# Hybrid decoder trunk: the first modulation's sums, their place before the first units, and the early constants

## The chip, the cores and the metric

The kernel runs on one core of a Trainium2 chip. Its time is the device time of one execution in microseconds (us); the number compared is the median of several executions. One core has five engines with queues of their own: TensorE (PE, with its weight loads shown apart as PEld), VectorE (DVE), ScalarE (ACT), GpSimd (POOL) and SyncE (SP), which here issues nearly all transfers. Each engine works through its queue in order and waits on semaphores of the others.

## The reference

One layer over 2048 positions of width 1024, then a final RMSNorm. Six modulation vectors come first, from the conditioning vector `c`:

```python
c_act = jax.nn.silu(c)
mod = c_act @ ada_w[l] + ada_b[l]                  # (1024) @ (1024, 6 * 1024)
sh1, sc1, g1, sh2, sc2, g2 = jnp.split(mod, N_MOD, axis=-1)
h = rmsnorm(x, norm_mix_w[l]) * (1.0 + sc1) + sh1
proj = h @ w_in[l]
...   # gated recurrence, top-k sparse attention, convolution; each on a slice of proj
x = x + g1 * (concat(o_a, o_b, o_c) @ w_out[l])
h = rmsnorm(x, norm_mlp_w[l]) * (1.0 + sc2) + sh2
x = x + g2 * (square(relu(h @ mlp_w1[l])) @ mlp_w2[l])
return rmsnorm(x, final_norm_w)
```

The change is about `sh1` and `sc1` (in the kernel `a1 = (1 + sc1) * norm_mix_w`), each a product of a vector of 1024 and a matrix of 1024 x 1024, without which no column of `h` can be made.

## The kernel before

The positions are worked in four blocks of 512. Per block, `in_block` makes the scaled and shifted activations transposed (eight tiles `k` of 128 x 512) and multiplies them with the columns of `w_in`, a unit of 128 or 256 columns at a time. Each float32 product is made from rounded parts: `whi`, `wlo` of the weights and `ah`, `al` of the activations, three matmuls for one. A unit of 128 columns is 24 matmuls of 128x512. What the units give feeds queues of background work (recurrence, convolution, indexer, top-k, attention), a bit of each after each unit. Later stages are the output product and the two MLP products.

The start. `in_norm(0)` loads four tiles `xt` and scales them. `ada_half(sec, c0, ...)` makes 512 columns of one modulation vector: it loads eight tiles `adw` (128 x 512, 256 KB each, one for each `k`), multiplies each by column `k` of `cact` and adds them up over `k`; then TensorE sums over the partitions, four matmuls with a moving vector of one column for each tile (`part_sum`). Of the eight tiles, before, DVE takes six (into `adacc`); for the two in `AK` ACT multiplies and POOL adds, and their sum goes through `part_sum` with `ones`. The halves `c0 = 0` for `a1` and `sh1` are needed for the tiles `k` = 0 to 3, the halves `c0 = TB` for `k` = 4 to 7.

`to_act_steps` makes one activation tile per step: four PE transposes into PSUM, `tf` on ACT (scale `a1`, shift `sh1`), `ah` on ACT, `al = tf - ah` on DVE or POOL. `tf` has two buffers, so the third `tf` waits until the first `al` is made. `first_units` begins two units (`KO = 2`, accumulators `at`) with `k` = 0 to 3 and ends them with `k` = 4 to 7. A third unit follows (accumulator `mm`, before `mm_661`), then a fourth (`mm_707`).

Weights come into two buffers `wraw`, are split by ACT (`whi`) and POOL (`wlo`), into four buffers each, and both parts are also written to DRAM (`wk_d`) for the later blocks.

The order in which each engine's queue stands is set by a scheduler when the program is built: it places the instructions by an estimated timeline of its own, with the order of the code as priority. So a change at the start can also move instructions much later.

`late_consts`, called after the second unit in block 0, makes the constants of the top-k search (`search_consts`: a few DVE operations on 14 columns, two powers on POOL) and five level masks (`lmask`: ten selections on POOL over 256 columns each, five copies on DVE).

Of the kernel before, what the change touches and what calls it, by code (L numbers as in the profile page):

```python
# [8 lines left out]
F32 = mybir.dt.float32  # L9
# [32 lines left out]
VB, GB, ZB = 3, 2, 3  # L42
HUB, FBB, HPM = 1, 2, 0
KO, NPF = 2, 2
AK = [1, 2]
PTB, PM, LB, LB2 = 1, 1, 4, 4
PREP = 14
R1 = [1126, 1216, 1594]
# [30 lines left out]
def trunk(ctx, tc, x, c, ada_w, ada_b, norm_mix_w, norm_mlp_w, w_in, hg_lb_logits,  # L79
# [136 lines left out]
    def ada_half(sec, c0, dst, key, slots):  # L216
        acc = hp.tile([P, TB], F32, tag="cu", bufs=2, name=nm("adacc"))
        pt = ps_ax()
        n = TB // P
        t0 = c0 // P  # L220

        side = []

        def part_sum(t, vec, first, last):
            for i in range(n):
                T.matmul(pt[:, i:i + 1], t[:, i * P:(i + 1) * P], vec, start=(first and i == 0),
                         stop=last, skip_group_check=True)

        for k in range(NK):
            t = slots[k]()  # L230
            dma(t, ada2[k * P:(k + 1) * P, sec * D + c0:sec * D + c0 + TB])
            if k in AK:
                A.mul(t, t, cact[:, k:k + 1])
                side.append(t)
                if len(side) > 1:
                    G.tensor_tensor(side[0], side[0], t, OP.add)
            elif k == 0:
                V.tensor_scalar(acc, t, cact[:, 0:1], None, op0=OP.mult)
            else:
                V.scalar_tensor_tensor(acc, t, cact[:, k:k + 1], acc, op0=OP.mult, op1=OP.add)  # L240
        if side:
            part_sum(side[0], ones[:, 0:1], True, False)
        part_sum(acc, ones[:, 0:1], not side, True)
        V.tensor_tensor(dst[:, t0:t0 + n], pt[:, :n], col("adab", sec * 8 + t0, n), OP.add)
        if key is not None:
            part = slice(c0 // P, (c0 + TB) // P)
            V.scalar_tensor_tensor(dst[:, part], dst[:, part], 1.0, cols[:, offs[key] + part.start:offs[key] + part.stop],
                                   op0=OP.add, op1=OP.mult)
# [23 lines left out]
        for i, j in zip(cuts, cuts[1:]):  # L272
            e.tensor_tensor(lo[:, i:j], src[:, i:j], hi[:, i:j].bitcast(F32), OP.subtract)  # L273

    def to_act_steps(xh, acol, bcol, ah, al, mid=None):
        for k in range(NK):
            guard = tc.high_priority(offset=HA)
            guard.__enter__()
            pt = {'0': ps_ax, '1': ps_mm, '2': ps_at, '3': ps_po}[(TA2 if px['ax'] < 3 else TA)[k]]()
            for t in range(4):  # L280
                T.transpose(pt[:, t * P:(t + 1) * P], xh[t][:, k * P:(k + 1) * P], ident)
            hi = ap.tile([P, TB], F32R, tag="ah", bufs=8, name=nm("ah"))
            lo = ap.tile([P, TB], F32R, tag="al", bufs=8, name=nm("al"))
            tf = xp.tile([P, TB], F32, tag="tf", bufs=2, name=nm("tf"))
            ac, bc = acol[:, k:k + 1], bcol[:, k:k + 1]
            A.activation(tf, pt, AF.Identity, scale=ac, bias=bc)  # L286
            A.copy(hi, tf)
            (V if k in (1, 4, 6) else G).tensor_tensor(lo, tf, hi.bitcast(F32), OP.subtract)
            guard.__exit__(None, None, None)
            ah.append(hi)  # L290
            al.append(lo)
            if mid is not None and k % 2:
                mid()
            yield
# [171 lines left out]
    def search_consts():  # L466
# [23 lines left out]
        G.iota(i8i, pattern=[[1, 8]], base=0, channel_multiplier=0)  # L490
        V.tensor_scalar(i8, i8i, 0.5, None, op0=OP.add)

    def late_consts():
        search_consts()
        cvrow = hp.tile([TAPS, 256], F32, tag="hc0", bufs=1, name="cvrow")
        nc.scalar.dma_start(cvrow, cv_w[0])
        pt = ps_ax()
# [7 lines left out]
        V.tensor_tensor(lbt, lbt, lbc, OP.mult)  # L505
        V.tensor_tensor(lbc, lbt, lbt, OP.subtract)
        V.tensor_scalar(oml, lbc, -1.0, 1.0, op0=OP.mult, op1=OP.add)

        mwork = hp.tile([P, 256], F32, tag="r", bufs=1, name="mwork")
        for l in range(5):  # L510
            h = 1 << l
            ng = 128 // (2 * h)
            V.memset(mwork, 1.0)
            G.affine_select(mwork, mwork, pattern=[[0, 4], [-2 * h, ng], [0, h]],
                            compare_op=OP.is_ge, fill=0.0, base=0, channel_multiplier=1)
            G.affine_select(mwork, mwork, pattern=[[0, 4], [2 * h, ng], [0, h]],
                            compare_op=OP.is_gt, fill=0.0, base=h, channel_multiplier=-1)
            V.tensor_copy(lmask[:, l, :], mwork)

    def ev_index_k(b, ps):  # L520
        full = st("stg", STG)
# [578 lines left out]

    def first_units(xts):
        act = [], []
        steps = to_act_steps(xts, a1, sh1, *act)
        ws = []
        for k in range(NK // 2):
            next(steps)
        for u in range(KO):
            ws.append(next_w())
            early.append(ps_at())
            mm_T(early[u], ws[u], act, True, None, 0, NK // 2)  # L1110
        ada_half(1, TB, a1, "nmix", far)
        ada_half(0, TB, sh1, None, far2)
        for _ in steps:
            pass
        for u in range(KO):
# [473 lines left out]
    far = [slot("f", ZB), slot("k", ZB), slot("q", ZB)] * 2 + [slot("v", VB), slot("gate", GB)]  # L1589
    far2 = [slot("f", ZB), slot("k", ZB), slot("q", ZB), slot("v", VB), slot("gate", GB)]  # L1590
    far2 += [slot("at", 2), slot("at", 2), slot("u", 2)]
    xq = [in_norm(0)]
    ada_half(1, 0, a1, "nmix", near)
    ada_half(0, 0, sh1, None, near)
# [74 lines left out]
```

## Time and profile before

| what | value |
|---|---|
| median of 3 runs (lowest to highest) | 2895.05 us (2892.56 to 2900.15) |
| the profiled execution | 2887.88 us, its span 2886.1 us |
| PE busy over the span | 2757.0 us, 96% |
| PE busy from 0 to 70 us | 40.40 us |
| PE busy from 70 to 200 us | 126.97 us |
| DVE, ACT, POOL busy over the span | 58%, 43%, 38% |
| mean granted TensorE clock | 0.987 |

Starts are counted in us from the first instruction. A row of the timeline reads: start, duration, engine, line, operation, output<-input, shapes, how many; in brackets the idle time ahead of it and what ended it. A float32 matmul of the kind of `part_sum` leaves two records, so four of them stand as x8.

### The profile page before, as it was taken

How to read it: one execution, taken by the hardware profiler on the slowest of the kernel's cores; microseconds unless marked ns; L12 is line 12 of the kernel's file. 1: busy time of each engine (PE TensorE's matmuls, PEld its weight loads, DVE VectorE, ACT ScalarE, POOL GpSimd, SP SyncE). 2: the span in 40 equal slices, each digit the busy share in tenths (PEclk: the TensorE clock that was granted, in tenths of full speed). 3: DMA queues.
4: the chain of work that ended last, by engine and by line, in shares of the span. 5: the costliest groups of instructions: out<-in, count | busy, mean ns of one | idle time of the engine just before them, and what ended most of it. 6: DMA issues, size and time to landing. Idle time of an engine off the chain costs nothing.

```text
span 2886.1 us, 42799 instructions
## 1 busy us (share of the span) xinstructions
PE 2757.0 (96%) x14116; PEld 2297.4 (80%) x14116; DVE 1671.6 (58%) x3514; ACT 1240.7 (43%) x2630; POOL 1086.6 (38%) x1051
## 2 busy tenths in 40 slices
PE   5999998999999989999999999999999999999997
PEld 4888887888788777888777888888788887777876
DVE  6695697777465437657757637477662221254455
ACT  4436444533311354555556444354643333343333
POOL 7434111212100445666665222234422223345444
PEclk9999999999999989999999999999999999999999
DMA  8987676777555667889888776677867666686676
GB/s 292 293 270 248 216 233 195 221 222 248 190 187 179 224 223 252 282 287 288 291 271 290 237 223 213 208 248 257 285 219 234 204 225 204 219 283 210 229 238 207
DMA packets 428075, 688.62 MB, mean 239 GB/s; under 512 B 43384, under 2 KB 171453, under 8 KB 427837
## 3 DMA queue, kind: packets, MB, share of 16 engines
q1 hardware_dynamic: 427680, 685.67, 73.0%
q8 instruction: 113, 1.85, 0.3%
q14 instruction: 126, 1.02, 0.1%
q10 hardware_dynamic: 156, 0.07, 0.0%
HBM read 532.74 MB, written 152.84 MB: 238 GB/s over the span
## 4 chain that ended last, share of the span: by engine, by line
PE 45%; DMA 4%; DVE 4%; POOL 2%; issue 1%; ACT 1%; SPq 0%; POOLq 0%; DVEq 0%; ACTq 0%
PE mm L1306 11%; PE mm L424 10%; PE ax L424 7%; PE ax L1306 6%; PE mm L1466 3%; PE at L967 2%; PE po L1001 2%; PE at L989 1%; PE ix L809 1%; DMA wk<-wk_d 1%; DMA tr<-in_mlp_w_dram 1%; PE at L1306 1%; DVE s L816 1%; POOL wk L376 1%; DVE cum L919 1%
## 5 line engine op out<-in xcount | busy, mean ns | idle before, releaser
L424 PE MATMUL mm<-ah,wk 128*128 128x512 f32 x1920 | 509.4, 396 | 4.9 <-ACT tf L286 1.9
L424 PEld LDWEIGHTS mm<-ah,wk 128*128 128x128 f32 x1920 | 353.6, 188 | 77.7 <-ACT tf L286 2.1
L318 POOL TENSOR_TENSOR wlo<-wraw,whi 128x512 fp32r<-128x512 f32 x210 | 286.7, 1385 | 243.4 <-ACT whi L317 99.7
L999 POOL TENSOR_TENSOR pT<-L,pT 128x512 fp32r<-128x512 f32 (+3 forms) x160 | 192.9, 1207 | 371.8 <-ACT pT L998 203.1
L816 DVE SCALAR_TENSOR_TENSOR s<-r,iw_s,s 128x512 f32<-128x512 f32 (+3 forms) x266 | 237.4, 892 | 100.9 <-ACT r L811 92.8
L424 PE MATMUL mm<-al,wk 128*128 128x512 f32 x960 | 262.3, 395 | 0.0
L969 DVE CUSTOM_DVE_ANT_0 L<-at,bias 128x512 f32<-128x512 f32 (+3 forms) x152 | 93.7, 620 | 202.5 <-PE at L967 159.3
L424 PEld LDWEIGHTS mm<-al,wk 128*128 128x128 f32 x960 | 177.9, 188 | 35.4
L1306 PE MATMUL mm<-wk,hh 128*128 128x512 f32 x640 | 196.0, 395 | 2.1 <-ACT tf L286 1.1
L811 ACT ACTIVATE r<-ix 128x512 f32<-128x512 f32 (+3 forms) x256 | 133.3, 555 | 148.8 <-PE ix L809 99.9
L317 ACT CAST whi<-wraw 128x512 fp32r<-128x512 f32 x210 | 121.8, 621 | 159.7 <-DMA wraw<-in_mlp_w_dram 40.1
L273 POOL TENSOR_TENSOR hl<-hr,hh 128x512 fp32r<-128x512 f32 x96 | 128.5, 1340 | 159.9 <-ACT hh L265 158.1
L424 PE MATMUL ax<-ah,wk 128*128 128x512 f32 x720 | 185.4, 391 | 1.8 <-ACT hc L1440 1.4
L589 DVE SCALAR_TENSOR_TENSOR cx<-hc,cvc,cx 128x512 f32<-128x512 f32 x232 | 174.2, 751 | 2.0
L919 DVE TENSOR_SCALAR_CACHE_REDUCE cum<-s,ssm 128x384 bf16<-128x384 f32 (+13 forms) x112 | 165.4, 1477 | 8.2 <-POOL s L820 6.1
L997 ACT COPY L<-at 128x512 f32<-128x512 f32 (+3 forms) x160 | 82.9, 522 | 175.6 <-PE at L989 174.2
L424 PEld LDWEIGHTS ax<-ah,wk 128*128 128x128 f32 x720 | 134.1, 188 | 30.2 <-ACT hc L1440 1.8
L1466 PE MATMUL mm<-wk,hc 128*128 128x512 f32 x588 | 145.0, 392 | 6.9 <-DVE acc L1474 6.1
L983 ACT ACTIVATE L<-L,nmx 128x512 f32<-128x512 f32 (+3 forms) x160 | 103.8, 650 | 98.7 <-DVE nmx L978 98.4
L1306 PEld LDWEIGHTS mm<-wk,hh 128*128 128x128 f32 x640 | 118.0, 188 | 26.8 <-ACT tf L286 1.7
L1466 PEld LDWEIGHTS mm<-wk,hc 128*128 128x128 f32 x588 | 109.4, 188 | 34.1 <-DVE acc L1474 10.0
L1306 PE MATMUL ax<-wk,hh 128*128 128x512 f32 x384 | 122.6, 397 | 1.5 <-DMA wk<-wk_d 1.1
(364 smaller groups left out, 6077.8 us busy)
## 6 DMA issues: line engine op xcount, KB each, us to landing
wk<-wk_d SPq DMA_DIRECT2D x776, 256.0 KB
wk<-wk_d SPq DMA_DIRECT2D x196, 512.0 KB
wk_d<-whi SPq DMA_DIRECT2D x210, 256.0 KB
wk_d<-wlo SPq DMA_DIRECT2D x210, 256.0 KB
wraw<-in_mlp_w_dram SPq DMA_DIRECT2D x68, 512.0 KB
kc<-sk_d SPq DMA_DIRECT2D x112, 256.0 KB
vc<-v_d SPq DMA_DIRECT2D x112, 256.0 KB
adw<-in_ada_w_dram SPq DMA_DIRECT2D x128, 128.0 KB
```

Source lines behind the costliest of these rows:

```text
L273: e.tensor_tensor(lo[:, i:j], src[:, i:j], hi[:, i:j].bitcast(F32), OP.subtract)
L317: A.copy(hi, src)
L318: G.tensor_tensor(lo, src, hi.bitcast(F32), OP.subtract)
L424: T.matmul(ps, ww[k], aa[k], start=(n == 0 and k0 == 0), stop=(n == len(order) - 1 and k1 == NK))
L589: V.scalar_tensor_tensor(acc if w < TAPS - 1 else total, hc[:, w:w + TB], cvc[:, m, w:w + 1], acc, op0=OP.mult, op1=OP.add)
L811: A.activation(r[:, :w], ps[:, :w], AF.Relu, scale=32.0 ** -0.5)
L816: V.scalar_tensor_tensor(s[:, c0:c0 + w], r[:, :w], iw, s[:, c0:c0 + w], op0=OP.mult, op1=OP.add)
L919: V.tensor_scalar(dump, s, t, -AIM - i * STEP, op0=OP.is_ge, op1=OP.add, accum_out=d)
L983: A.activation(lt[:, :w], lt[:, :w], AF.Exp, bias=nmx, accum_out=sm[:, cb:cb + 1])
L999: G.tensor_tensor(pT[:, :nt, 1], lv, pT[:, :nt, 0].bitcast(F32), OP.subtract)
L1306: T.matmul(ps, aa[f][:, tok * P:(tok + 1) * P], ww[i], start=(first and n == 0), stop=(last and n == 5))
L1466: T.matmul(bank[t], aa[:, k, t * P:(t + 1) * P], ww[k], start=(i in (0, 2, 4) and n == 0), stop=(n == 5), skip_group_check=True)
```

## The change

Four edits:

- `AK` is `[2, 5]` instead of `[1, 2]`, and for these two of the eight tiles TensorE multiplies by `cact` itself: `part_sum(t, cact[:, k])` accumulates into the same PSUM tile. ACT's eight multiplications and POOL's four additions go; each of the four halves has twelve `part_sum` matmuls instead of eight.
- The two `ada_half` calls for the second half stand ahead of the first two units in `first_units`, no longer behind their first half.
- In block 0, all eight `al` are made on DVE, before three of eight (the other blocks keep 1, 4, 6).
- `search_consts` and the level masks (now `level_masks`, 64 columns selected and copied four times) stand at the very start, ahead of the load of `x`, no longer in `late_consts`.

```diff
-AK = [1, 2]
+AK = [2, 5]
...
             if k in AK:
-                A.mul(t, t, cact[:, k:k + 1])
-                side.append(t)
-                if len(side) > 1:
-                    G.tensor_tensor(side[0], side[0], t, OP.add)
+                part_sum(t, cact[:, k:k + 1], k == AK[0], False)
...
-        if side:
-            part_sum(side[0], ones[:, 0:1], True, False)
-        part_sum(acc, ones[:, 0:1], not side, True)
+        part_sum(acc, ones[:, 0:1], False, True)
...
-            (V if k in (1, 4, 6) else G).tensor_tensor(lo, tf, hi.bitcast(F32), OP.subtract)
+            (V if k in on_v else G).tensor_tensor(lo, tf, hi.bitcast(F32), OP.subtract)
...
+    def level_masks():
+        mwork = hp.tile([P, 5, 64], F32, tag="r", bufs=1, name="mwork")
+        V.memset(mwork, 1.0)
+        for l in range(5):
...
+            G.affine_select(mwork[:, l], mwork[:, l], pattern=[[-2 * h, ng], [0, h]],
...
+        for c in range(4):
+            V.tensor_copy(lmask[:, :, c * 64:(c + 1) * 64], mwork)
...
     def late_consts():
-        search_consts()
...
     def first_units(xts):
         act = [], []
-        steps = to_act_steps(xts, a1, sh1, *act)
+        steps = to_act_steps(xts, a1, sh1, *act, None, range(NK))
         ws = []
         for k in range(NK // 2):
             next(steps)
+        ada_half(1, TB, a1, "nmix", far)
+        ada_half(0, TB, sh1, None, far2)
         for u in range(KO):
             ws.append(next_w())
             early.append(ps_at())
             mm_T(early[u], ws[u], act, True, None, 0, NK // 2)
-        ada_half(1, TB, a1, "nmix", far)
-        ada_half(0, TB, sh1, None, far2)
...
+    search_consts()
+    level_masks()
     xq = [in_norm(0)]
```

What the scheduler makes of it, at three places. First PE's queue at the second half's sums: `adacc_427`, `adw_469`, `adacc_464` are the second half before (`ax_428` for `a1`, `ax_465` for `sh1`), `adacc_413`, `adw_459`, `adw_471`, `adacc_451` the same now (`ax_414`, `ax_452`); `at_...` are the matmuls of the first two units, `mm_511` and `mm_542` transposes of the second half. Before:

```order
L226 MATMUL ax_428<-ones,adacc_427 128x1
L424 MATMUL at_391<-al_368,whi_375 128x512
L424 MATMUL at_391<-ah_367,wlo_376 128x512
L424 MATMUL at_414<-al_368,whi_383 128x512
L424 MATMUL at_414<-ah_367,wlo_384 128x512
L226 MATMUL ax_465<-ones,adw_469 128x1 x4
L226 MATMUL ax_465<-ones,adacc_464 128x1 x4
L281 MATMUL mm_511<-ident,xt_213 128x128
```

Now, on the same engine at the same work:

```order
L274 MATMUL mm_542<-ident,xt_251 128x128
L417 MATMUL at_506<-al_397,whi_490 128x512
L224 MATMUL ax_414<-ones,adacc_413 128x1 x4
L224 MATMUL ax_452<-cact,adw_459 128x1 x4
L224 MATMUL ax_452<-cact,adw_471 128x1 x4
L224 MATMUL ax_452<-ones,adacc_451 128x1 x4
L417 MATMUL at_506<-ah_396,wlo_491 128x512
L417 MATMUL at_506<-ah_407,whi_490 128x512
```

The last sum of the modulation has moved ahead of nine matmuls of the units' first half (`at_506`, `at_529`, with `k` = 2 and 3), which before stood ahead of it.

Second, DVE's queue in the second half of the modulation (`adacc_427` then `adacc_464` before, `adacc_413` then `adacc_451` now; `al_346` and `al_375` to `al_408` are the low parts of `k` = 0 to 3). Before:

```order
L518 CAST lmask<-mwork 128x256
L240 SCALAR_TENSOR_TENSOR adacc_427<-adw_439,cact,adacc_427 128x512
L240 SCALAR_TENSOR_TENSOR adacc_427<-adw_442,cact,adacc_427 128x512
L240 SCALAR_TENSOR_TENSOR adacc_427<-adw_445,cact,adacc_427 128x512
L288 TENSOR_TENSOR al_346<-tf_347,ah_345 128x512
L240 SCALAR_TENSOR_TENSOR adacc_427<-adw_448,cact,adacc_427 128x512
L238 TENSOR_SCALAR adacc_464<-adw_466,cact 128x512
L240 SCALAR_TENSOR_TENSOR adacc_427<-adw_451,cact,adacc_427 128x512
L240 SCALAR_TENSOR_TENSOR adacc_464<-adw_476,cact,adacc_464 128x512
```

Now:

```order
L235 SCALAR_TENSOR_TENSOR adacc_413<-adw_427,cact,adacc_413 128x512
L281 TENSOR_TENSOR al_375<-tf_376,ah_374 128x512
L281 TENSOR_TENSOR al_386<-tf_387,ah_385 128x512
L235 SCALAR_TENSOR_TENSOR adacc_413<-adw_430,cact,adacc_413 128x512
L235 SCALAR_TENSOR_TENSOR adacc_413<-adw_439,cact,adacc_413 128x512
L281 TENSOR_TENSOR al_397<-tf_398,ah_396 128x512
L235 SCALAR_TENSOR_TENSOR adacc_413<-adw_442,cact,adacc_413 128x512
L233 TENSOR_SCALAR adacc_451<-adw_453,cact 128x512
L281 TENSOR_TENSOR al_408<-tf_409,ah_407 128x512
L235 SCALAR_TENSOR_TENSOR adacc_451<-adw_456,cact,adacc_451 128x512
```

All four low parts now stand between the twelve modulation steps, before one did; the masks and search constants are gone from here.

Third, POOL's queue from the third of the four first weight splits (`wlo`) on. Before:

```order
L318 TENSOR_TENSOR wlo_384<-wraw_327,whi_383 128x512
L318 TENSOR_TENSOR wlo_388<-wraw_327,whi_387 128x512
L236 TENSOR_TENSOR adw_432<-adw_432,adw_435 128x512
L288 TENSOR_TENSOR al_335<-tf_336,ah_334 128x512
L288 TENSOR_TENSOR al_357<-tf_358,ah_356 128x512
L236 TENSOR_TENSOR adw_469<-adw_469,adw_472 128x512
L288 TENSOR_TENSOR al_368<-tf_369,ah_367 128x512
L479 TENSOR_TENSOR sconst<-sconst 128x14
```

Now:

```order
L311 TENSOR_TENSOR wlo_499<-wraw_367,whi_498 128x512
L311 TENSOR_TENSOR wlo_503<-wraw_367,whi_502 128x512
L311 TENSOR_TENSOR wlo_522<-wraw_488,whi_521 128x512
L311 TENSOR_TENSOR wlo_526<-wraw_488,whi_525 128x512
L247 TENSOR_SCALAR rs_2326<-ss_2324 128x1
```

Between the splits of the first two units and those of the third, POOL has nothing left to do.

More of the change, by code (lines that the diff above doesn't have):

```diff
@@ L220, in ada_half @@
         t0 = c0 // P
-        side = []
         def part_sum(t, vec, first, last):
@@ L273, in low_part, with to_act_steps @@
             e.tensor_tensor(lo[:, i:j], src[:, i:j], hi[:, i:j].bitcast(F32), OP.subtract)
-    def to_act_steps(xh, acol, bcol, ah, al, mid=None):
+    def to_act_steps(xh, acol, bcol, ah, al, mid=None, on_v=(1, 4, 6)):
         for k in range(NK):
@@ L491, in search_consts @@
         V.tensor_scalar(i8, i8i, 0.5, None, op0=OP.add)
+    def level_masks():
+        mwork = hp.tile([P, 5, 64], F32, tag="r", bufs=1, name="mwork")
+        V.memset(mwork, 1.0)
+        for l in range(5):
+            h = 1 << l
+            ng = 128 // (2 * h)
+            G.affine_select(mwork[:, l], mwork[:, l], pattern=[[-2 * h, ng], [0, h]],
+                            compare_op=OP.is_ge, fill=0.0, base=0, channel_multiplier=1)
+            G.affine_select(mwork[:, l], mwork[:, l], pattern=[[2 * h, ng], [0, h]],
+                            compare_op=OP.is_gt, fill=0.0, base=h, channel_multiplier=-1)
+        for c in range(4):
+            V.tensor_copy(lmask[:, :, c * 64:(c + 1) * 64], mwork)
     def late_consts():
-        search_consts()
         cvrow = hp.tile([TAPS, 256], F32, tag="hc0", bufs=1, name="cvrow")
@@ L507, in late_consts @@
         V.tensor_scalar(oml, lbc, -1.0, 1.0, op0=OP.mult, op1=OP.add)
[L509 to L518, printed above, removed]
     def ev_index_k(b, ps):
```

## The prediction, as it was put on record

> **What bounds the kernel now.** I read the page first, then the busy times by stage, then those of the first 120 us, and then each engine's timeline from 20 to 70 us. The columns behind the stretch are its length, busy time (records) of PE, PEld, DVE, ACT and POOL, granted clock, DMA share, GB/s.
>
> ```profile
> span 2886.1 us, 42799 instructions
> core 0: us, PE busy (x) PEld busy (x) DVE busy (x) ACT busy (x) POOL busy (x), PEclk, DMA share, GB/s
> 0.00:70.00 70.00, 40.40 (x173) 32.81 (x174) 47.65 (x92) 34.01 (x57) 51.47 (x54) 0.98 0.89 291
> 70.00:200.00 130.00, 126.97 (x706) 109.91 (x705) 99.39 (x242) 51.00 (x103) 59.02 (x52) 0.99 0.87 276
> 200.00:1000.00 800.00, 772.62 (x4683) 663.76 (x4683) 538.80 (x1317) 312.51 (x732) 168.61 (x204) 0.99 0.68 217
> 1000.00:2886.00 1886.00, 1816.98 (x8560) 1490.90 (x8558) 985.70 (x1864) 843.21 (x1739) 807.51 (x742) 0.99 0.74 243
> ```
>
> From 70 us on PE is idle only 3.0 + 27.4 + 69.0 us of 2816; before that it is idle 29.6 of 70. So what a change of the start is worth is how much earlier PE becomes busy for good; everything later hangs on PE and moves with it, but for what the DMA queue cannot bring earlier. When does that happen, and what is it waiting for?
>
> ```profile
> 30.52 0.16 DVE L244 TENSOR_TENSOR sh<-ax,cols 128x4 f32<-128x4 f32 x1 [1.40 <-PE ax L226]
> 50.19 0.16 DVE L244 TENSOR_TENSOR sh<-ax,cols 128x4 f32<-128x4 f32 x1 [0.91 <-PE ax L226]
> ...
> 27.94 1.14 ACT L317 CAST whi<-wraw 128x512 fp32r<-128x512 f32 x2 [1.15 <-DMA wraw<-in_w_in_dram]
> 30.78 1.45 ACT L286 ACTIVATE tf<-mm,sh,a 128x512 f32<-128x512 f32 x2 [1.70 <-DVE sh L244]
> 39.38 0.78 ACT L286 ACTIVATE tf<-mm,sh,a 128x512 f32<-128x512 f32 x1 [4.91 <-DVE al L288]
> 58.70 0.78 ACT L286 ACTIVATE tf<-mm,sh,a 128x512 f32<-128x512 f32 x1 [4.04 <-DVE gq__210 L488]
> 59.51 0.62 ACT L287 CAST ah<-tf 128x512 fp32r<-128x512 f32 x1
> ...
> 60.17 0.50 PE L424 MATMUL mm<-ah,whi 128*128 128x512 f32 x1 [3.75 <-ACT ah L287]
> 69.44 1.98 PE L424 MATMUL mm<-ah,whi 128*128 128x512 f32 x8
> ```
>
> The reader is to see a chain: first half of the modulation done at 30.7, second half at 50.35, last activation tile `ah` at 60.13, and from there PE never stops. Unit four (mm_707) begins at 69.44; that is my checkpoint. Two stalls stand on the chain besides the modulation: `tf` waits 4.91 us for a low part, and 4.04 us for DVE's search constants. Why the second half comes only at 50:
>
> ```profile
> 28.75 0.37 DVE L238 TENSOR_SCALAR adacc<-adw,cact 128x512 f32<-128x512 f32 x1
> 32.50 5.11 DVE L240 SCALAR_TENSOR_TENSOR adacc<-adw,cact,adacc 128x512 f32<-128x512 f32 x3
> 37.53 1.75 DVE L288 TENSOR_TENSOR al<-tf,ah 128x512 fp32r<-128x512 f32 x1
> 40.27 7.26 DVE L240 SCALAR_TENSOR_TENSOR adacc<-adw,cact,adacc 128x512 f32<-128x512 f32 x6
> ...
> 31.17 4.22 POOL L318 TENSOR_TENSOR wlo<-wraw,whi 128x512 fp32r<-128x512 f32 x3
> 35.35 1.71 POOL L236 TENSOR_TENSOR adw<-adw,adw 128x512 f32<-128x512 f32 x1
> 37.02 1.72 POOL L288 TENSOR_TENSOR al<-tf,ah 128x512 fp32r<-128x512 f32 x1
> 48.78 2.60 POOL L479 TENSOR_TENSOR sconst<-sconst 128x14 f32<-128x14 f32 x1 [2.59 <-DVE sconst L476]
> ...
> L240 DVE SCALAR_TENSOR_TENSOR adacc<-adw,cact,adacc x20: 716/750/1758, 12.8 to 46.8; 128x512 f32<-128x512 f32 x20
> L288 DVE TENSOR_TENSOR al<-tf,ah x3: 683/691/1754, 37.5 to 57.9; 128x512 fp32r<-128x512 f32 x3
> ```
>
> DVE works without a break from 28.75 to 47.5, and beside POOL's tensor_tensor its steps take 1.70 us (5.11 for three) where the median is 0.75.
>
> **The change part by part.**
>
> *First half, TensorE's quarter.* The eight ACT multiplications and four POOL additions go; DVE keeps its six tiles a half. `tf` at 30.78 waited 1.70 us for `sh`; ahead of it on ACT stand the weight casts, which end at 29.08 and wait for DMA, whose issue order is the same now. So the gain here is between 0 and 1.7 us. I take 1.7, since DVE no longer waits between its steps for POOL's masks.
>
> *The early constants.* POOL now does ten selections of 64 columns and two powers at the start, instead of ten selections of 256 spread over it:
>
> ```profile
> 2.17 2.12 POOL L514 TENSOR_SCALAR_AFFINE_SELECT mwork<-mwork 128x256 f32<-128x256 f32 x1
> ```
>
> At most ten of this row are 21 us, at a quarter each 5.3, beside 5.2 for the two powers at 2.60; POOL is then free for `rs` (the norm of `x`) between 12.7 and, at worst, 28. The transposes need the scaled `x` by 29: hidden, so I cost it at nothing; the worst end would cost about 2 us. What it takes away is the 4.04 us wait at 58.70.
>
> *Second half ahead of the units, all low parts on DVE.* DVE now owes from about 28.3: ten steps of 0.75, two of 0.4, four `al` of 0.69, that is 11.1 us; about two of them run beside POOL's remaining `wlo` and take 1.70 (2.0 more). The end is 41.4, against 47.5. It cannot be before the last tile lands. Landed by then must be 4 x 0.52 MB of x, 32 x 0.26 of ada_w and 1.05 of weights, 11.6 MB:
>
> ```profile
> 0.00:10.00 10.00, 0.24 (x1) 0.17 (x1) 1.97 (x15) 2.20 (x3) 6.86 (x13) 1.00 0.79 273
> 10.00:20.00 10.00, 3.15 (x13) 2.57 (x13) 7.35 (x15) 7.65 (x14) 9.04 (x11) 1.00 0.93 321
> 20.00:30.00 10.00, 6.08 (x28) 5.48 (x27) 8.54 (x17) 2.34 (x5) 6.03 (x7) 1.00 0.98 269
> 30.00:40.00 10.00, 5.53 (x21) 4.24 (x20) 8.87 (x8) 4.32 (x7) 8.73 (x7) 1.00 1.06 390
> ```
>
> 8.63 MB by 30 us and 0.39 MB per us after: 37.6. So the sums are DVE's, with 3.8 us to the floor. PE then does four matmuls:
>
> ```profile
> 31.61 1.97 PE L281 MATMUL mm<-ident,xt 128*128 128x128 f32 x8 [1.13 <-ACT tf L286]
> 28.62 1.86 PE L226 MATMUL ax<-ones,adacc 128*128 128x1 f32 x8 [2.89 <-DVE adacc L240]
> 49.12 1.03 PE L226 MATMUL ax<-ones,adacc 128*128 128x1 f32 x8
> 41.55 0.63 PE L424 MATMUL at<-ah,wlo 128*128 128x512 f32 x1
> 41.98 0.63 PE L424 MATMUL at<-ah,whi 128*128 128x512 f32 x1
> 44.17 0.39 PE L424 MATMUL at<-ah,whi 128*128 128x512 f32 x1
> 44.41 0.40 PE L424 MATMUL at<-al,whi 128*128 128x512 f32 x1
> 62.00:64.00 2.00, 2.00 (x6) 1.60 (x5) 0.75 (x1) 1.81 (x4) 0.45 (x2) 0.50 0.95 268
> ```
>
> PE's queue now holds the last sum ahead of nine unit matmuls, so it will have waited since about 38; after a wait of this kind the trace shows 0.43 us from matmul to matmul (41.55 to 41.98), later 0.24 (44.17 to 44.41), and 1.86 for the four small ones against 1.03. I take the slow ones: sums at 43.3, `sh` at 43.5, a gain of 6.8 (bounds: 10.5 at the DMA floor with quick sums; 5 if two more steps meet POOL). The sixteen more small matmuls lie in such waits but for the last eight, counted here.
>
> The granted clock behind the 3.75 us wait of before is 0.50 (62 to 64 us). The Trainium skill (TensorE: Matmul & The Clock Gate, Part 1) says that PE's clock halves after an idle window of about 3.4 us and is full again after as long of sustained work; that speaks against placing the last sum ahead of the nine matmuls. By it the next step costs what I take from the rows; without it the checkpoint would be 2.4 us earlier. The trace agrees at 62 us; at 41.98 its column says 1.00 where the matmuls are slow, so there the rows decide.
>
> *From `sh` to the checkpoint.* Ahead of the first `tf` of the second half now stand, on PE, the nine matmuls (0.43 each) and seven transposes (0.25, eight in 1.97): 43.3 + 3.9 + 1.7 = 48.9. Two `tf` (1.45 as at 30.78) and two `ah` (1.14 as the casts at 27.94) follow; the first `ah` is at 50.9, its `al` on DVE at 51.6, and as DVE has no constants in between, the last `ah` at 54.3 (60.13 before, with the 4.04 in it). PE is busy for good from 51.6: 46 matmuls at 0.227 (eight take 1.98 us, the last 0.39 of it: 1.59 in seven steps) bring unit four at 62.1. Against 69.44 that is 7.3 us.
>
> *The transfers.* They must do in 62 us what they did in 69.4.
>
> ```profile
> 104.24 1.14 ACT L317 CAST whi<-wraw 128x512 fp32r<-128x512 f32 x2 [3.05 <-DMA wraw<-in_w_in_dram]
> 100.00:110.00 10.00, 10.00 (x51) 8.57 (x50) 8.56 (x15) 4.16 (x9) 5.82 (x4) 1.00 0.99 299
> ```
>
> 20.2 MB (291 GB/s x 69.4) against 12.5 MB by 40 us and 22 us at 0.33 (between the rows' 0.30 and 0.39): about 0.4 MB short, 1.1 at 0.30, so 1 to 3.5 us of backlog, part of it x for the next block that nobody awaits. The split at 104.24 waits for DMA, just ahead of its use. I take 1 us off, with 0 and 3.5 as bounds. Sum: 7.3 - 1 = 6.3, say 6.5 us with the small relief of DVE behind it. On the profiled execution 2886.1 - 6.5 = 2879.6 us of span, 2881.4 with the 1.8 around it; the median of the runs is 7.2 above the profiled execution, so 2895.05 - 6.5 = 2888.5.
>
> **The rivals.**
>
> *Quick clock and no cover lost.* If PE stays at full clock there, unit four comes 2.4 us earlier, and if the DVE steps meet POOL less, up to 3 more. Against it: the slow rows at 41.55. Gain 9 to 13, 2882 to 2886.
>
> *DMA takes it back.* If each unit's weights come at the pace of the saturated queue (share 0.99 at 100 to 110), unit four begins when 20.2 MB have come, 12.5 by 40 us and the rest at 0.30 MB/us: 66 us, a gain of 3.5, or 1 to 4 with what waits behind it, 2891 to 2894. Against it: PE is 10.00 of 10 there and never waited.
>
> *Slower.* The scheduler writes the queues of blocks 0 to 3 in another order. PE is idle 27.4 us from 200 to 1000, in small waits, and DVE is 538.8 of 800 busy there. If the new order puts PE's matmuls ahead of the DVE results they need, these waits grow; they must reach 43 us (27.4 + 6.5 + 8.7) for a slower kernel: 2904 or more. For it: nothing binds this order to what DVE can do. Against it: the order of the work is the code's, only shifted.
>
> **How the numbers follow.** A difference under 0.3%, 8.7 us, cannot be told from none. Forecast (gain 4 to 9) 0.45, of which 0.05 is over 8.7; quick 0.32; DMA 0.12; slower 0.11, of which 0.02 is within 0.3%. That makes faster 0.37, same 0.54, slower 0.09. The range goes from a gain of 13 (2882) to a loss of 3 (2898): it leaves out the slower rival and a little of the quick one.
>
> **What would show it.** `sh` of the second half near 43.5, last `ah` near 54, unit four near 62, and PE idle from 70 to 1000 about 30 us as before: right. `sh` before 41 says the contention was over-counted; matmuls at 0.24 right after the last sum, that the clock was. If the checkpoint is early and the end is not, the waits between 200 and 1000 or casts waiting for `wraw` took it.

## The result, and the profile after

The changed kernel takes 2918.15 us (median of 6 runs, 2914.95 to 2920.16); the kernel before takes 2897.6 beside it on the same chip (6 runs, 2884.49 to 2903.12). The ratio is 1.0071, 95% interval 1.0055 to 1.0087: slower by 20.5 us, where the prediction was 6.5 us faster and its range ended at 2898.

The busy times by stage of the changed kernel (columns as in the prediction: PE, PEld, DVE, ACT, POOL, granted clock, DMA share, GB/s):

```profile
span 2918.5 us, 42856 instructions
0.00:70.00 70.00, 49.53 (x228) 42.55 (x229) 43.65 (x92) 28.76 (x49) 30.03 (x46) 0.95 0.91 302
70.00:200.00 130.00, 122.31 (x677) 105.18 (x676) 100.57 (x246) 51.07 (x102) 53.15 (x49) 0.97 0.85 264
200.00:1000.00 800.00, 766.92 (x4580) 659.17 (x4579) 533.10 (x1299) 311.70 (x727) 152.21 (x195) 0.97 0.66 211
```

The start is better: PE is busy 49.5 us of the first 70, before 40.4. From 70 to 200 us PE is idle 7.7 us instead of 3.0, from 200 to 1000 33.1 instead of 27.4, and the granted clock there is 0.97 instead of 0.99. Two things follow: PE waits 10.4 us more (40.8 against 30.4), and it is slower while it works.

To see where the time goes I matched every TensorE instruction of the two profiled executions (same line, same tiles, same count) and took the start after minus the start before, the median in each stretch of the kernel before:

| stretch of before, us | 75–150 | 200–450 | 500–550 | 600–675 | 800–1000 |
|---|---|---|---|---|---|
| lag of the changed kernel, us | -2.7 | +1.7 | +3.7 | +8.6 | +20.3 |

So the start's gain is 2.7 us at 75 us, and 23.0 us are lost between 150 and 760 us; from there to 1000 us the lag does not move. For the work between 150 and 760 us PE waits 25.1 us before and 33.8 now (there 147.3 to 780.4 us), so waits explain 8.7 of these 23.0; the other 1.7 of the 10.4 lie ahead of it, at 73 us. The remaining 14.3 is the same matmuls taking longer. The trace's clock records show half clock (granted clock 0.50) for 51.2 us between 70 and 1000 us (nine stretches), before for 17.1 (four), and all of these lie between 150 and 765 us. The split is that of two single executions, and that of before has little half clock: the two other kernels below with its queues have 27.3 and 34.1 us of it.

(The profiled executions differ by 32.3 us in all. That of before, 2887.88, stands 9.7 under the median beside it, that of the changed kernel 2.0 over its own; 9.7 + 2.0 + 20.5 is the 32.3. Behind 1000 us the lag grows by another 9 us; it also grows by 7 us or more in two of the kernels below that are not slower, the fill on the kernel before and TensorE's quarter alone.)

The waits of PE from 70 to 1000 us, summed by what PE waited for (total, times, longest), first the kernel before, then the changed one:

```profile
PE mm L281 <- ACT tf L286: 5.8, 7, 1.8
PE ax L671 <- DVE r L751: 4.6, 4, 3.0
...
PE ax L696 <- DVE k L662: 1.6, 2, 1.0
...
```

```profile
PE mm L274 <- ACT tf L279: 6.4, 7, 1.7
PE mm L417 <- DVE slo L535: 6.0, 1, 6.0
PE at L1007 <- POOL ot L1005: 3.4, 2, 3.1
PE ax L690 <- DVE k L656: 3.2, 2, 2.5
...
```

Three long waits are new: 6.0 us for `slo`, 3.1 for `ot`, 2.5 for `k`. All three come from the new order: something late stands ahead of what PE needs, or what PE needs hangs on a transfer that has moved back. The first, in the changed kernel on DVE and PE, and behind it a window of busy time:

```profile
164.29 0.14 DVE L927 CAST far<-at 1x1 uint32<-1x1 f32 x1
170.01 1.50 DVE L872 SCALAR_TENSOR_TENSOR s<-cum,s 128x384 f32<-128x384 bf16 x1 [4.84 <-DVEq L930]
175.81 0.68 DVE L535 SCALAR_TENSOR_TENSOR slo<-mm,shi 128x512 fp32r<-128x512 f32 x1
176.55 3.78 PE L417 MATMUL mm<-ah,whi 128*128 128x512 f32 x8 [5.98 <-DVE slo L535]
176.50:182.50 6.00, 5.95 (x14) 4.75 (x15) 6.00 (x18) 0.38 (x1) 0.00 (x0) 0.50 0.58 171
```

L930 is a branch on a value that the search computes (`far`); DVE stands 4.84 us there. `slo` frees the PSUM bank (a part of the memory into which PE writes its sums) that PE needs next, and in the new order it stands behind the branch and behind a piece of the search, so PE waits 5.98 us; then eight matmuls take 3.78 us instead of 1.98 at clock 0.50. In the kernel before, `slo` stands ahead of its branch and is done 9 us earlier:

```profile
166.96 0.68 DVE L541 SCALAR_TENSOR_TENSOR slo<-mm,shi 128x512 fp32r<-128x512 f32 x1
176.75 0.56 DVE L878 SCALAR_TENSOR_TENSOR s<-cum,s 128x384 f32<-128x384 bf16 x1 [5.80 <-DVEq L936]
```

The second, at 575 us: on ACT a load of its function table (1.28 us) and a `cu` of the convolution stand right ahead of the copy `ot`, which POOL and then PE need:

```profile
573.76 0.72 ACT L615 ACTIVATE cu<-cacc,cols 128x512 f32<-128x512 f32 x1
575.33 0.48 PE L1007 MATMUL at<-ident,ot 128*128 128x128 f32 x1 [3.06 <-POOL ot L1005]
```

In the kernel before, this `cu` stands ahead of the exponentials `L` and not between them and `ot`, and PE does not wait for `ot`:

```profile
562.88 0.74 ACT L621 ACTIVATE cu<-cacc,cols 128x512 f32<-128x512 f32 x1
567.98 0.27 PE L1013 MATMUL at<-ident,ot 128*128 128x128 f32 x1
```

The third, at 725 us: on ACT a cast of a transfer that has not landed (`mh`) stands ahead of the copies `v`; DVE's low part of `v` waits for that copy, and `k`, which PE needs, stands behind this low part in DVE's queue.

```profile
715.61 1.40 SPq L107 DMA_DIRECT2D mr<-mx_d  x3
720.09 1.30 ACT L258 CAST mh<-mr 128x512 fp32r<-128x512 f32 x2 [8.96 <-DMA mr<-mx_d]
721.29 0.26 ACT L557 CAST v<-mm 128x128 fp32r<-128x128 f32 x1
721.58 0.29 DVE L558 TENSOR_TENSOR v<-mm,v 128x128 fp32r<-128x128 f32 x1 [5.75 <-ACT v L557]
725.13 1.87 PE L690 MATMUL ax<-q,k 128*128 128x64 f32 x8 [2.54 <-DVE k L656]
731.20 3.76 PE L417 MATMUL mm<-ah,wk 128*128 128x512 f32 x8
```

In the kernel before, casts `mh` stand ahead of copies `v` too, but the transfer comes much earlier: SP issues the first `mr` at 685.57 us, 30.0 us earlier than in the changed kernel, though PE's lag there is only about 10 us. In SP's queue `mr` stands right behind the writing of an attention output (`mx_d<-ot`), which goes out at 684.68 us before and at 714.07 now; before, it stands ahead of the writing of the recurrence's `r` (693.55), now behind it (703.92). PE runs through the same place (711.74 to 714.90 us) without a wait, and the eight matmuls take 2.09 us:

```profile
685.57 1.50 SPq L107 DMA_DIRECT2D mr<-mx_d  x3
711.74 1.00 PE L696 MATMUL ax<-q,k 128*128 128x64 f32 x8
714.90 2.09 PE L424 MATMUL mm<-ah,wk 128*128 128x512 f32 x8
```

### The profile page after: what moved, and what is told of

Read it like the earlier page. It is cut to its first block, busy times and chain, and to the rows that moved or that the text cites. A ratio compares the mean times of both kernels' runs of the same rounds, so it can differ in the third digit from the quotient of the medians.

```text
span 2918.5 us, 42856 instructions
## 1 busy us (share of the span) xinstructions
PE 2780.4 (95%) x14148; PEld 2317.9 (79%) x14148; DVE 1674.7 (57%) x3514; ACT 1240.0 (42%) x2626; POOL 1061.2 (36%) x1042
## 3 DMA queue, kind: packets, MB, share of 16 engines
q8 instruction: 113, 1.85, 0.3%
## 4 chain that ended last, share of the span: by engine, by line
PE 42%; DMA 5%; DVE 3%; POOL 1%; issue 1%; ACT 1%; SPq 0%; POOLq 0%; DVEq 0%; ACTq 0%
PE mm L1300 10%; PE mm L417 9%; PE ax L417 7%; PE ax L1300 6%; PE mm L1460 4%; DMA wk<-wk_d 2%; PE at L961 1%; PE po L995 1%; PE at L983 1%; PE ix L803 1%; DMA tr<-in_mlp_w_dram 1%; PE at L1300 1%; POOL wk L369 1%; DVE cum L913 1%; DVE s L810 0%
```

## The experiments

The theory: what the change computes costs nothing; the scheduler answers it with another order of the queues in blocks 0 to 3, and this order costs the 20 us, by waits and by the half clock behind them. The first rival: a part of the content (TensorE's quarter, the second half ahead, the low parts on DVE, the early constants) carries the loss. To measure how far an order has moved I count the matmuls of the queue of PE that are out of the order of another kernel (of some 13,300); the changed kernel has 768 out of the order of before.

**A fill that moves the order, on the changed kernel** (`lmask` is overwritten later; 242 matmuls out of the order of before, about 750 out of that of the changed kernel):

```diff
     i8 = cst.tile([P, 8], F32, name="i8")
+    V.memset(lmask, 0.0)
```

> The changed kernel with one more DVE memset at the start, of the level masks' tile, which is written in full later: it costs nothing where DVE waits for c, but the scheduler then writes the queues of blocks 0 to 3 nearly as in the kernel before (242 of 13,338 PE matmuls out of the old order, against 768). Theory 'order' (the loss is the other order of the queues behind the start): 2888 to 2900 us, unit four still near 65 us, PE idle from 70 to 1000 us near 30 us and the clock at half for some 20 us there. Rival 'content' (the earlier start, the low parts on DVE or the extra matmuls themselves cost it): 2912 to 2922 us, as the changed kernel.

Measured: 2896.1 us (2888.43 to 2902.01) against 2895.99, ratio 1.0002 (0.9986 to 1.0018). With all of the change and one instruction more, the loss is gone. In part the forecast missed: PE waits 36.3 us from 70 to 1000 us, not some 30, and stands at half clock for 10.2, not some 20. The `slo` is back ahead of the branch, PE does not wait for it, and the stage reads:

```profile
164.00 0.68 DVE L536 SCALAR_TENSOR_TENSOR slo<-mm,shi 128x512 fp32r<-128x512 f32 x1
166.84 0.14 DVE L928 CAST far<-at 1x1 uint32<-1x1 f32 x1
70.00:200.00 130.00, 127.39 (x715) 110.09 (x714) 104.44 (x250) 51.43 (x104) 58.68 (x50) 1.00 0.89 280
```

**The same fill on the kernel before** (840 matmuls moved):

> The kernel before with the same one memset, nothing else: its queues change about as much as by the change under study (840 PE matmuls out of order). Theory 'order': a time that differs from the kernel before by more than the memset can cost (under 2 us), most likely 2902 to 2920 us, with the start (unit four at 69.4 us) unchanged; a change to the faster side would also speak for it. Rival 'content': 2893 to 2902 us, as before.

Measured: 2896.73 us (2892.85 to 2902.2), ratio 0.9999 (0.9986 to 1.0012). The forecast missed: I expected a loss from the order, and by itself this time is the rival's. An order that is moved further than that of the changed kernel costs nothing here: not the moving costs, but what stands where.

**A fill that does not move the order**, the control for the first one:

```diff
     i8 = cst.tile([P, 8], F32, name="i8")
+    V.memset(zq, 0.0)
```

> The changed kernel with one small fill at the start (14 columns of `zq`, overwritten later), a control for the first run with a fill. This fill leaves the queues as they stand in the changed kernel (no matmul out of its place). Theory (the order of the queues makes the loss): 2914 to 2921 us, ratio 1.006 to 1.009, and near 725 us the same wait of 2.5 us with TensorE at half clock for about 10 us behind it. Rival (a fill at the start helps by itself, whatever the order): about 2896, as with the fill of `lmask`.

Measured: 2917.13 us (2910.53 to 2920.68), ratio 1.0070 (1.0050 to 1.0091). A fill as such helps nothing; the theory holds. The wait at 725 us is there again, with the same queues, but the half clock behind it is shorter than I expected (see below).

**The change without the early constants:**

```diff
     def late_consts():
+        search_consts()
...
-    search_consts()
-    level_masks()
     xq = [in_norm(0)]
```

> Three of the four edits (TensorE's quarter, the second half ahead of the units, low parts on DVE), with the constants and masks where they were; its queues stand near the old order (166 PE matmuls moved). 'Order': 2888 to 2900 us. 'Content': 2908 to 2922 us, unless the early constants are what costs.

Measured: 2901.4 us (2893.1 to 2904.64), ratio 1.0014 (1.0000 to 1.0028). It does not have the loss of 20 us, though it lies 1.4 us above the range of 'order'. Up to 75 us it is ahead of the kernel before (last `ah` ends at 57.61, before at 60.13); then PE waits 4.86 us for a `slo`, which itself waits for ACT's `shi`, and the lag at 75–150 us is +4.6:

```profile
56.99 0.62 ACT L280 CAST ah<-tf 128x512 fp32r<-128x512 f32 x1
76.62 0.69 DVE L531 TENSOR_TENSOR slo<-mm,shi 128x512 fp32r<-128x512 f32 x1 [1.62 <-ACT shi L530]
77.37 3.78 PE L417 MATMUL mm<-ah,whi 128*128 128x512 f32 x8 [4.86 <-DVE slo L531]
```

**The early constants alone**, on the kernel before:

```diff
     def late_consts():
-        search_consts()
...
+    search_consts()
+    level_masks()
     xq = [in_norm(0)]
```

> Only the early constants and masks, the other three edits left out; 223 PE matmuls out of the old order. 'Order': within 8 us of the kernel before, 2889 to 2905 us, unit four 1 to 4 us earlier than 69.4 since the wait of 4.04 us for the search constants goes. 'Content' with the early constants as its cause: 2910 us or more.

Measured: 2889.41 us (2882.91 to 2896.67), ratio 0.9978 (0.9963 to 0.9992): faster than both kernels by a small edit. The lag at 75–150 us is -5.4, twice the gain of the whole change. PE is busy without a gap from 70 to 200 us, and the last `ah` ends at 51.37:

```profile
70.00:200.00 130.00, 130.00 (x727) 112.59 (x726) 103.37 (x248) 48.91 (x100) 57.95 (x51) 0.99 0.89 281
50.75 0.62 ACT L287 CAST ah<-tf 128x512 fp32r<-128x512 f32 x1
```

**The parts one by one**, on the kernel before or taken out of the changed kernel. TensorE's quarter alone, on the kernel before:

```diff
-AK = [1, 2]
+AK = [2, 5]
...
-                A.mul(t, t, cact[:, k:k + 1])
+                part_sum(t, cact[:, k:k + 1], k == AK[0], False)
...
```

> The kernel before, with TensorE's quarter of the sums as the only edit (`AK` = [2, 5], `part_sum` with `cact`). Its queues stand far from both (799 matmuls out of the order of before, 882 out of that of the changed kernel). Theory (order): the quarter's own gain lies in the first 70 us, at most 2 us, since the early constants are missing; what the new order costs later cannot be told beforehand, and it shows as waits with half clock behind them: 2893 to 2916, and the loss between 150 and 1000 us equal to about the added waits plus half of the added time at half clock. Rival (the quarter's sixteen further small matmuls, or its part_sums that hold up TensorE's queue, carry the loss): behind by 10 us or more already at 70 us, 2906 or more.

Measured: 2892.52 us (2888.44 to 2901.32), ratio 0.9995 (0.9983 to 1.0006), lag at 75–150 us -4.1. My bound of 2 us for the gain in the start was too low, and the time lies just under the range; the rival is out.

The quarter with the early constants (both diffs above):

> The kernel before with TensorE's quarter and the early constants; the second half stays behind the units in the code, and the low parts stay divided. The order is nearer to that of before (433 matmuls out of place) than to that of the changed kernel (706). Theory (order): start ahead by 5 to 6 us as with the constants alone, 2886 to 2896. Rival (the quarter costs about 20 us wherever the constants come early): 2910 or more.

Measured: 2893.55 us (2890.36 to 2900.74), ratio 0.9995 (0.9983 to 1.0007), lag at 75–150 us -4.3. The time is as expected of the order; the start is a little less ahead than the 5 to 6 us.

All but the quarter, that is the changed kernel with

```diff
-AK = [2, 5]
+AK = [1, 2]
...
-                part_sum(t, cact[:, k:k + 1], k == AK[0], False)
+                A.mul(t, t, cact[:, k:k + 1])
...
```

> The changed kernel without TensorE's quarter (ACT multiplies and POOL adds as before); the second half ahead of the units, all low parts on DVE, early constants. The queues stand as with the constants alone but for some 18 matmuls. Theory (order): as the constants alone, 2885 to 2893, with the start ahead by 5 to 8 us. Rival (the second half ahead, or all low parts on DVE, carries the loss): 2910 or more.

Measured: 2890.7 us (2884.86 to 2899.35), ratio 0.9982 (0.9966 to 0.9997), lag at 75–150 us -5.6. As expected of the order.

The second half ahead, alone, on the kernel before:

```diff
+        ada_half(1, TB, a1, "nmix", far)
+        ada_half(0, TB, sh1, None, far2)
         for u in range(KO):
...
-        ada_half(1, TB, a1, "nmix", far)
-        ada_half(0, TB, sh1, None, far2)
```

> The kernel before with one edit: the second half's two `ada_half` calls ahead of the first two units. Theory (the start's gain comes from the early constants; what comes later is the order, 334 matmuls out of the order of before): start ahead by 0 to 2 us at 75 to 150 us, 2893 to 2900 in all. Rival (the second half ahead is what makes the start early, as the prediction had it): ahead by 4 us or more at 75 to 150 us, 2888 to 2893.

Measured: 2890.53 us (2883.49 to 2900.25), ratio 0.9978 (0.9962 to 0.9994), faster than I expected and in the rival's range; but the lag at 75–150 us is +0.9, so the start did not come earlier by it, and the gain is not explained. DVE stands only 0.77 us at the first branch there, 5.80 before, and the lag falls to -2.0 at 200–450 us; but at 800–1000 us it is +5.5, so this profile does not show the gain.

All of the change, with the second half's calls put back behind the units:

```diff
-        ada_half(1, TB, a1, "nmix", far)
-        ada_half(0, TB, sh1, None, far2)
         for u in range(KO):
...
+        ada_half(1, TB, a1, "nmix", far)
+        ada_half(0, TB, sh1, None, far2)
```

> The changed kernel with the second half's two calls put back behind the first two units; all else of the change stays. In the code only these two lines stand elsewhere, but the queues stand in a third order (852 matmuls out of that of the changed kernel, 808 out of that of before). Theory (the changed kernel's order is a bad one among several, and the content costs nothing): 2887 to 2900, start ahead by 4 to 6 us at 75 to 150 us, and fewer waits of 1 us or more between 70 and 1000 us than the 14 of the changed kernel. Rival (TensorE's quarter with all low parts on DVE and early constants together overload DVE between 150 and 760 us, in whatever order): 2910 or more.

Measured: 2892.56 us (2887.68 to 2898.33), ratio 0.9990 (0.9977 to 1.0003), lag at 75–150 us -5.9, nine waits of 1 us or more. As expected: the same load on DVE, no loss. Here, too, a `slo` stands behind a branch (at 159.38 us, after 4.71 us), and PE does not wait for it: the place in the queue costs only if PE needs the result by then. In seven kernels that hold parts of the change or all of it but two moved lines, no part carries the loss.

**One place taken away, at 725 us.** In block 2 the eight copies `v` go to DVE; up to about 700 us the queues stay as in the changed kernel:

```diff
-                A.copy(v1[:, i, :, :64], src)
+                (V.tensor_copy if b == 2 else A.copy)(v1[:, i, :, :64], src)
```

> The changed kernel with one edit in block 2: the eight copies `v` (L557) are made on DVE instead of ACT, so that they no longer stand in ACT's queue behind a cast `mh` that waits for `mr`. Up to about 700 us the queues stay as in the changed kernel. Theory (each place where the order puts a late result ahead of a needed one costs its wait and the half clock behind it; the place at 725 us makes the lag grow from about 11 to about 20 us): the wait of 2.5 us ahead of `ax<-q,k` and the half clock behind it go, the lag against before stays at about 11 to 13 us from 760 us on, and the median is 2907 to 2912. Rival one (the matmuls of that stretch wait for the transfer `mr` in any case): a wait of the same size a few us further, lag about 20 and 2914 to 2921. Rival two (the whole loss hangs on the early places, and the later lag is noise of one execution): 2914 to 2921 as well, but without a wait there.

Measured: 2915.94 us (2911.76 to 2919.27), ratio 1.0074 (1.0049 to 1.0100). The theory missed here. Instead of 2.5 us PE waits 1.44 and, a little further, 1.85, and the lag is +19.7 at 800–1000 us all the same:

```profile
729.74 1.08 PE L690 MATMUL ax<-q,k 128*128 128x64 f32 x8 [1.44 <-DVE k L656]
742.35 1.00 DVE L199 SCALAR_TENSOR_TENSOR adacc<-adw,cact,adacc 128x256 f32<-128x256 f32 x2 [8.22 <-DMA adw<-in_ada_w_dram]
744.16 0.65 PE L698 MATMUL ax<-q,k 128*64 128x64 f32 x8 [1.85 <-DVE k L656]
```

The second is of the kind of rival one, with another transfer: DVE stands 8.22 us on a sum whose `adw` has not landed, and `k` stands behind it. The control, the same edit on the kernel before:

> The same edit (block 2's eight copies `v` on DVE) on the kernel before, as a control: its queues stay as they are (one matmul out of its place). Theory: PE does not wait at this place in the kernel before, so nothing changes, 2893 to 2899, ratio 0.999 to 1.001. Rival (the edit gains by itself, wherever the order puts it): 2885 to 2890, and then the gain of the run beside it says nothing on the order.

Measured: 2903.51 us (2892.14 to 2910.5), ratio 1.0025 (1.0008 to 1.0042). The forecast of no change missed: the edit has a price of its own, of about 7 us by the ratio, so the pair cannot say what the place at 725 us is worth. That the eight copies on DVE are the cause is not shown: in the profile the lag is already +5.7 at 600–675 us, ahead of them.

**One place taken away, at 176 us.** ACT copies the unit's result out of PSUM, so that the bank does not wait for `slo`. All queues stay as in the changed kernel (no matmul moves; 7 instructions on DVE and on ACT):

```diff
     def ev_sq(b, m, ps):
+        if b == 0 and m == 0:
+            full = st("stg", STG)
+            A.mul(full, ps, 0.125)
+            ps = full
-        for s, tl in enumerate(split_out(ps, 0.125)):
+        for s, tl in enumerate(split_out(ps, None if b == 0 and m == 0 else 0.125)):
```

> The changed kernel with one edit in block 0, first `ev_sq`: ACT copies the unit's result, scaled by 0.125, out of PSUM first, and `shi` and `slo` are made from the copy, so that the PSUM bank no longer waits for DVE's `slo`. All five queues stay as in the changed kernel (no matmul moves, DVE 7 and ACT 7 instructions). Theory (at 176 us PE waits 5.98 us because the new order puts this `slo` behind the branch at L930, and TensorE then stands at half clock for 6.8 us): wait and half clock go, the lag against before at 200 to 450 us falls from +2 to between -3 and -1, and the gain is kept to the end: 4 to 7 us less than the changed kernel, 2911 to 2914, about a quarter of the loss; the rest stays, at 500 to 580 and at 700 to 760 us. Rival one (PE meets another late result a few us further, such as `r<-ax` at 178 us): lag at 200 to 450 unchanged, 2916 to 2921. Rival two (the early stall brings on the later ones): the whole loss goes, 2893 to 2902.

Measured: 2916.28 us (2911.23 to 2921.28), ratio 1.0070 (1.0052 to 1.0088). Rival one: PE runs on to the next matmul that needs DVE and waits there, 5.02 us instead of 5.98.

```profile
170.25 1.60 DVE L876 SCALAR_TENSOR_TENSOR s<-cum,s 128x384 f32<-128x384 bf16 x1 [5.67 <-DVEq L934]
179.22 0.73 DVE L749 SCALAR_TENSOR_TENSOR r<-ax,cols,gate 128x512 f32<-128x512 f32 x1
180.01 1.65 PE L669 MATMUL ax<-q,k 128*128 128x192 f32 x4 [5.02 <-DVE r L749]
```

The control on the kernel before:

> The same edit on the kernel before, as a control (its `slo` stands ahead of the branch, and PE does not wait for it; no matmul moves). Theory: no change, 2892 to 2898, ratio 0.999 to 1.001. Rival (the edit has a gain or a price of its own): 2 us or more away, and that much has to be taken off the run beside it.

Measured: 2896.83 us (2889.16 to 2906.93), ratio 1.0006 (0.9988 to 1.0024). No change, as expected; the edit itself is free.

**All together.** Lags against the profiled execution of before, 800 to 1000 us, and from 70 to 1000 us PE's waits and its time at half clock:

| kernels | lag, us | waits, us | half clock, us | ratio to before |
|---|---|---|---|---|
| order of the changed kernel to at least 700 us (changed, small fill, `v` on DVE, bank freed) | +18.1 to +20.3 | 38.0 to 41.7 | 47.8 to 58.0 | 1.0070 to 1.0074 |
| any other order (eleven kernels, two of them with the order of before) | -3.0 to +9.4 | 29.3 to 36.3 | 10.2 to 44.4 | 0.9978 to 1.0025 |

One execution tells the lag no closer than several us: the control with the queues of before and a free edit reads +7.7 there, with a ratio of 1.0006. The gap between the two rows is beyond that. That the order makes the loss is shown; that it does so by waits and half clock together fits the table, in which only the four slow kernels have much of both (36.3 us of waits came with 10.2 at half clock, 44.4 at half clock with 32.3 of waits, and neither kernel has the loss). How it divides among its places is not: both attempts to take away one wait met the next one. At 176 us the trace says why: DVE as a whole comes late out of the branch, and there is no single instruction that PE could be freed of. Why the scheduler chose this order, and why one fill takes it away, was not tried.

## Why the prediction was wrong

*The first half.* Predicted gain 1.7 us; `tf` starts at 29.01 instead of 30.78. Right.

*The second half's sums.* Predicted `sh` at 43.5. The profile shows 42.54 + 0.16 = 42.7. DVE's last step ends at 41.40 (37.50 + 3.90), where the working had it; the last four sums take 1.05 us instead of the 1.86 that I took. Behind them PE's spacing is 0.43 us, as I took it from the slow rows, but not for my reason. I had PE wait since about 38; it was busy without a gap, and its clock halved all the same, behind the sums. That this size came out right was luck.

```profile
39.64 1.93 PE L224 MATMUL ax<-cact,adw 128*128 128x1 f32 x16
41.45 1.05 PE L224 MATMUL ax<-ones,adacc 128*128 128x1 f32 x8
42.54 0.16 DVE L237 TENSOR_TENSOR sh<-ax,cols 128x4 f32<-128x4 f32 x1 [0.88 <-PE ax L224]
36.00:42.50 6.50, 6.50 (x51) 6.11 (x50) 5.49 (x10) 0.13 (x1) 0.00 (x0) 1.00 1.04 343
42.50:46.00 3.50, 3.50 (x10) 2.71 (x10) 0.16 (x1) 0.62 (x1) 0.45 (x1) 0.51 1.08 353
```

*Last `ah`.* Predicted 54.3, measured 55.07 (53.93 + 1.14). Near, but two errors cancel. The first `tf` starts at 47.06, not 48.9 (the sums were early, and seven transposes took 0.93 us instead of 1.7), and its `ah` is done at about 49.0, not 50.9. But DVE had sums of the next modulation vector (L199) ahead of the low part, which waited 0.88 and 1.14 us for their transfers, so that `al` begins only at 51.81.

```profile
51.41 0.48 DVE L199 SCALAR_TENSOR_TENSOR adacc<-adw,cact,adacc 128x256 f32<-128x256 f32 x1 [1.14 <-DMA adw<-in_ada_w_dram]
52.55 0.61 PE L417 MATMUL at<-al,whi 128*128 128x512 f32 x1 [2.75 <-DVE al L281]
53.93 1.14 ACT L280 CAST ah<-tf 128x512 fp32r<-128x512 f32 x2
64.73 1.98 PE L417 MATMUL mm<-ah,whi 128*128 128x512 f32 x8
72.94 2.14 PE L417 MATMUL mm<-ah,whi 128*128 128x512 f32 x8 [1.68 <-DVE slo L532]
```

*The checkpoint.* Predicted 62.1, measured 64.73: a gain of 4.7 us, not 7.3. I let PE run at 0.227 us per matmul from 51.6 on. It began for good only at 52.55, after a wait of 2.75 us for that low part, and ran at 0.43 until 56.2. At 72.94 another 1.68 us go, for a `slo` whose `shi` stands on ACT behind a wait of 4.71 us for a transfer (`ki_d`). What is left at 75 us is 2.7 us; of the rivals, this is nearest to "DMA takes it back", whose gain was 1 to 4, although the transfers acted through the queues of DVE and ACT and not through the weights.

*Where the gain of the start comes from.* I gave it to the second half's earlier place and to the low parts on DVE, with 4.04 of it the constants. The runs show otherwise: constants alone 5.4 us at 75–150 us, TensorE's quarter alone 4.1, second half ahead alone none. The parts do not add up, and the low parts were not run alone.

*Two slips of the working* change nothing: the tiles that must have landed add up to 11.5 MB, not 11.6, and DVE was not without a break from 28.75 us, since its row at 30.52 shows 1.40 us of idle time.

*The failed step* is the sentence "everything later hangs on PE and moves with it", and with it the rival "Slower" and its 0.11. Its mechanism is what happened: the queues of blocks 0 to 3 stand in another order, and PE's matmuls stand ahead of the DVE results they need. Its price was wrong. I asked that the waits from 200 to 1000 us grow to 43 us for a slower kernel; they grew only to 33.1, with 7.7 instead of 3.0 ahead of them, and the kernel is 20 us slower. Left out were the matmuls at half clock behind the waits, in this pair of executions 14.3 of the 23.0 us lost, though the prediction itself had quoted such a place at 62 us. The condition "PE idle from 70 to 1000 about 30 us" reads 40.8. At what this kernel lost for each us of added waiting (23.0 by 8.7, or 2.6), the 15.2 us that the rival had to lose need 5.8 us of waits: the point from which it decides was near 33 us, not 43.

The Trainium skill (TensorE: Matmul & The Clock Gate, section "HAM oscillation — how this bites in real kernels") prices throttled time at half its length. By it the 34.1 us more at half clock would cost an estimated 17 us; what the waits leave over is 14.3, somewhat under the rule.

The other argument against that rival, that the order of the work is the code's and only shifted, was not one that a row of the trace supported. The order of the changed kernel could be read beforehand: 768 matmuls out of place, and `slo` behind the branch instead of ahead of it.

## What to carry to other kernels

Where a scheduler sets the queues, an edit is two edits: what it computes, and the order it brings about; compare the queues before costing the first, above all which results that free a PSUM bank have moved behind a branch or behind an instruction that waits for a transfer. Price a new wait of PE by its length and by the half clock behind it. When a change that ought to gain loses, run it once more with a neutral instruction that moves the order, and once with one that does not; the pair tells content from order.

## What was not expected of the hardware

Waits of 2.45 to 2.94 us at the place of 725 us were followed by very different times at half clock, with the same queues: 10.2 us in the changed kernel, 6.8 with the bank freed, 3.4 with the small fill. Windows of busy time with the granted clock in the third column from the right, the changed kernel first, then the small fill:

```profile
725.20:728.60 3.40, 3.40 (x16) 3.18 (x17) 1.38 (x4) 1.50 (x3) 1.96 (x2) 0.50 0.88 217
728.60:732.00 3.40, 3.40 (x13) 2.45 (x13) 2.07 (x7) 0.80 (x3) 0.66 (x1) 0.50 0.92 347
732.00:735.40 3.40, 3.40 (x9) 2.63 (x9) 1.07 (x4) 1.40 (x3) 1.60 (x2) 0.50 1.05 392
```

```profile
727.26 1.22 PE L691 MATMUL ax<-q,k 128*128 128x64 f32 x8 [2.45 <-DVE k L657]
730.70:734.10 3.40, 3.40 (x18) 2.80 (x18) 2.61 (x9) 0.53 (x2) 0.76 (x1) 0.89 0.99 358
```

The stretches come in steps of about 3.4 us, and PE was busy throughout them. The Trainium skill (TensorE: Matmul & The Clock Gate, Part 1) says that the clock halves after an idle window of about 3.4 us and is full again after one busy window, and that the window runs freely; here a wait of 2.5 us was enough, and full work did not always end it after one window.

Nor does the clock need a wait. In the changed kernel it halved at 42.55 us for 3.4 us, though PE had been busy in all of the 3.4 us ahead; 28 of the 29 records of that stretch are matmuls of `part_sum`, which move one column. Six of the kernels show half clock there with no idle time ahead of it, all of them with TensorE's quarter; the prediction had costed these short matmuls at their own time alone.

DVE's stall at the branch was not expected either: 4.84 us at L930 in the changed kernel and 5.80 at L936 before, in which the whole queue of DVE stands. At the same first branch it is 4.7 to 6.1 us in ten of the sixteen kernels and 0.2 to 1.6 in six, among them the first fill (1.56). What decides is open, and so is how much of that kernel's recovery at this place is the shorter stall and how much the place of `slo`.
